# Row normalisation on one core: from two pools of 4-row tiles to an in-place ring of 16-row tiles

## The chip, the core and the metric

The kernel runs on one NeuronCore of one Trainium2 chip. Five engines matter here by name: DVE (the vector engine), ACT (the scalar engine), POOL, SP, which here only issues transfers, and PE, which has no work. Sixteen DMA engines of the core move data between the chip's main memory (HBM) and the core's memory (SBUF, 128 partitions). Two queues feed these sixteen engines: q1 carries what SP issues, q10 what ACT issues.

The metric is the device time of one execution in microseconds; the median of several runs is compared. A profile is one separate execution, and its span runs from the first to the last instruction.

## The reference

```python
batch, seq, dim = 32, 512, 1024            # x is float32

def reference(x, eps):                     # eps = 1e-5
    mean = np.mean(x, axis=-1, keepdims=True)
    var = np.var(x, axis=-1, keepdims=True)
    return ((x - mean) / np.sqrt(var + eps)).astype(np.float32)
```

There are 32 x 512 = 16384 rows of 1024 floats, 4 KB each. Every row is read once and written once: 67.11 MB in and 67.11 MB out.

## The kernel before

A tile is 512 rows, laid out as 128 partitions of K = 4 consecutive rows (line 30), so each partition holds 16 KB that lie together in HBM as well. There are 32 tiles. Two pools of six buffers each hold them: `xin` for what is loaded (line 35) and `yout` for what is stored (line 36). A tile therefore takes 16 KB a partition twice, and up to six tiles may be on their way in and six on their way out.

For each tile, in the loop of line 43:

- SP issues one load of 2 MB (line 47). From the seventh tile on it first waits until the buffer that it reuses is free, which is when DVE and ACT have read the tile six before it.
- DVE makes the statistics (lines 53 and 57): per row two `bn_stats` over 512 elements each and one `bn_aggr`, which gives mean and variance.
- DVE makes minus the mean (line 59), variance plus eps (line 61) and its reciprocal (line 65), each for four rows at once.
- ACT takes the square root of the reciprocal (line 68), which is the factor `rstd`.
- POOL multiplies minus the mean by `rstd` (line 71), which is the offset `nmr`.
- ACT makes the output with one instruction for each row, `yt = xt * rstd + nmr` (line 75), from the input buffer into the output buffer.
- ACT issues one store of 2 MB on its own queue (line 84).

The order on each engine is set by the scheduler of the tile framework, not by the text of the kernel. On ACT it often puts the square root of the next tile, or of the next two, ahead of the four row instructions of a tile. The framework gives each transfer one of eight completion semaphores in turn, and a transfer that reuses a semaphore waits until that semaphore's earlier transfer has landed.

Of the kernel before, what the change touches and what calls it, by code (L numbers as in the profile page):

```python
# [1 line left out]

# [4 lines left out]


@with_exitstack  # L10
def kernel(
    ctx: ExitStack,
    tc: tile.TileContext,
    x: bass.AP,
    eps: bass.AP,
    out: bass.AP,
):
    nc = tc.nc
    P = nc.NUM_PARTITIONS

    eps_val = float(eps) if not isinstance(eps, bass.AP) else 1e-5

    x2 = x.flatten_outer_dims()
    o2 = out.flatten_outer_dims()
    N, D = x2.shape
    BN_MAX = nc.vector.BN_STATS_FMAX
    assert D % BN_MAX == 0
    NSUB = D // BN_MAX

    K = 4  # L30
    rows_per_tile = P * K
    assert N % rows_per_tile == 0
    ntiles = N // rows_per_tile

    xin = ctx.enter_context(tc.tile_pool(name="xin", bufs=6))
    yout = ctx.enter_context(tc.tile_pool(name="yout", bufs=6))
    st = ctx.enter_context(tc.tile_pool(name="st", bufs=4))

    fdt = mybir.dt.float32
    AF = mybir.ActivationFunctionType  # L40
    ALU = mybir.AluOpType

    for t in range(ntiles):
        rows = slice(t * rows_per_tile, (t + 1) * rows_per_tile)

        xt = xin.tile([P, K, D], fdt)
        nc.sync.dma_start(out=xt, in_=x2[rows].rearrange("(p k) d -> p k d", p=P))  # L47

        stats = st.tile([P, K, NSUB, 6], fdt)
        mv = st.tile([P, K, 2], fdt)  # L50
        for k in range(K):
            for s in range(NSUB):
                nc.vector.bn_stats(  # L53
                    out=stats[:, k, s, :],
                    in_=xt[:, k, s * BN_MAX : (s + 1) * BN_MAX],
                )
            nc.vector.bn_aggr(out=mv[:, k, :], in_=stats[:, k, :, :])  # L57
        negmean = st.tile([P, K], fdt)
        nc.vector.tensor_scalar_mul(out=negmean, in0=mv[:, :, 0], scalar1=-1.0)  # L59
        vpe = st.tile([P, K], fdt)  # L60
        nc.vector.tensor_scalar(  # L61
            out=vpe, in0=mv[:, :, 1], scalar1=eps_val, scalar2=None, op0=ALU.add
        )
        ivar = st.tile([P, K], fdt)
        nc.vector.reciprocal(out=ivar, in_=vpe)  # L65

        rstd = st.tile([P, K], fdt)
        nc.scalar.activation(out=rstd, in_=ivar, func=AF.Sqrt, bias=0.0, scale=1.0)  # L68

        nmr = st.tile([P, K], fdt)  # L70
        nc.gpsimd.tensor_mul(out=nmr, in0=negmean, in1=rstd)  # L71

        yt = yout.tile([P, K, D], fdt)
        for k in range(K):
            nc.scalar.activation(  # L75
                out=yt[:, k, :],
                in_=xt[:, k, :],
                func=AF.Identity,
                bias=nmr[:, k : k + 1],
                scale=rstd[:, k : k + 1],  # L80
            )

        dst = o2[rows].rearrange("(p k) d -> p k d", p=P)
        nc.scalar.dma_start(out=dst, in_=yt)


# [1 line left out]
_INS = ['x', 'eps']  # L88
_OUTS = [((32, 512, 1024), 'float32')]
#: Inputs that are plain numbers.  # L90
_NUMBERS = {'eps': 1e-05}


# [26 lines left out]
```

## Time and profile before

| | before |
|---|---|
| runs (three): median, lowest to highest | 321.07 us, 320.96 to 321.11 us |
| profiled execution, span | 319.0 us |
| DVE busy | 181.6 us, 480 instructions |
| ACT busy | 154.3 us, 161 instructions |
| POOL busy | 6.6 us, 36 instructions |
| instructions in all | 926 |
| first `bn_stats` begins | 8.60 us |
| last row instruction of ACT ends | 309.3 us |
| SP's wait at the end for the last stores | part of 57.8 us that it waits for stores, 5 times |

The page of a profile gives the busy time of each engine, then the span in 40 equal slices, then the DMA queues, then the chain of work that ended last (followed back from the last instruction to what released it), then the costliest groups of instructions, and last the transfers by line, with the median time from issue to landing. Of the table, the first and the second row differ by 2.0 us: that lies outside the span, or is the difference between one execution and the others.

### The profile page before, as it was taken

What the parts mean: (1) busy time and instruction counts of PE and PEld (TensorE: products, weight loads), DVE (VectorE), ACT (ScalarE), POOL (GpSimd) and SP (SyncE); (2) the same over time, 40 slices, a digit from 0 to 9 for tenths busy, and PEclk for the clock granted to TensorE, in tenths of its full rate; (3) what the DMA queues carried; (4) which work ended last, traced back from release to release, by engine and by line L of the source; (5) the groups of instructions that cost most, each with busy time, mean ns of one, the idle gap of its engine ahead of it and who ended that gap; (6) DMA issues with size and microseconds to landing.
All of it is one profiled execution on the core that took longest, in us unless ns stands there. A gap on an engine that the chain in (4) does not pass through costs nothing.

```text
span 319.0 us, 926 instructions
## 1 busy us (share of the span) xinstructions
DVE 181.6 (57%) x480; ACT 154.3 (48%) x161; POOL 6.6 (2%) x36
## 2 busy tenths in 40 slices
DVE  0999764457754477544676355765446744467610
ACT  1147491651907419074380833809247091470970
POOL 0000000000000000000000000000000000000000
DMA  7999999999999999999999999999999999999995
GB/s 294 427 405 422 438 431 431 431 429 431 426 429 432 435 431 431 429 427 431 431 433 435 430 431 427 427 431 427 435 438 430 428 431 427 431 427 427 421 427 220
DMA packets 9222, 134.27 MB, mean 421 GB/s; under 512 B 1024, under 2 KB 1024, under 8 KB 1024
## 3 DMA queue, kind: packets, MB, share of 16 engines
q1 hardware_dynamic: 4608, 67.11, 49.6%
q10 hardware_dynamic: 4608, 67.11, 49.2%
q14 instruction: 6, 0.05, 0.0%
HBM read 67.11 MB, written 67.11 MB: 421 GB/s over the span
## 4 chain that ended last, share of the span: by engine, by line
DMA 87%; DVE 4%; issue 3%; ACT 2%; SPq 1%; POOLq 0%; POOL 0%; DVEq 0%
DMA xt<-in_x_dram 87%; DVE stats L53 3%; ACT yt L75 1%; SPq L47 1%; DVE mv L57 0%; DVE ivar L65 0%; DVE negmean L59 0%; POOLq L115 0%; ACT rstd L68 0%; POOL nmr L71 0%; DVE vpe L61 0%; DVEq L65 0%; DVEq L59 0%
## 5 line engine op out<-in xcount | busy, mean ns | idle before, releaser
L53 DVE BATCH_NORM_STATS2 stats<-xt 128x6 f32<-128x512 f32 x256 | 159.4, 665 | 115.3 <-DMA xt<-in_x_dram 115.3
L75 ACT ACTIVATE yt<-xt,nmr,rstd 128x1024 f32<-128x1024 f32 x128 | 146.7, 1227 | 4.7 <-POOL nmr L71 4.5
L68 ACT ACTIVATE rstd<-ivar 128x4 f32<-128x4 f32 x32 | 6.6, 205 | 149.6 <-DVE ivar L65 149.0
L57 DVE BATCH_NORM_AGGREGATE mv<-stats 128x2 f32<-128x12 f32 x128 | 25.1, 196 | 1.1
L71 POOL TENSOR_TENSOR nmr<-negmean,rstd 128x4 f32<-128x4 f32 x32 | 6.3, 198 | 297.9 <-ACT rstd L68 297.9
L65 DVE RECIPROCAL ivar<-vpe 128x4 f32<-128x4 f32 x32 | 5.7, 178 | 3.0
L59 DVE TENSOR_SCALAR negmean<-mv 128x4 f32<-128x4 f32 x32 | 5.4, 170 | 3.1
L61 DVE TENSOR_SCALAR vpe<-mv 128x4 f32<-128x4 f32 x32 | 5.2, 162 | 0.0
L68 ACT ACT_TABLE_LOAD x1 | 1.3, 1283 | 0.7 <-PEq L101 0.7
L101 POOL MEMSET const-float32-0.0<- 128x1 f32 x1 | 0.1, 98 | 0.2 <-issue 0.2
L101 POOL MEMSET const-uint8-127<- 128x1 uint8 x1 | 0.1, 102 | 0.0
L101 POOL MEMSET const-bfloat16-1.0<- 128x1 bf16 x1 | 0.1, 101 | 0.0
L101 POOL MEMSET const-float32-1.0<- 128x1 f32 x1 | 0.1, 98 | 0.0
## 6 DMA issues: line engine op xcount, KB each, us to landing
xt<-in_x_dram SPq DMA_DIRECT2D x32, 2048.0 KB, 38.4
out_dram<-yt ACTq DMA_DIRECT2D x32, 2048.0 KB, 15.5
```

Of the source, the lines that this page charges most:

```text
L47: nc.sync.dma_start(out=xt, in_=x2[rows].rearrange("(p k) d -> p k d", p=P))
L53: nc.vector.bn_stats(out=stats[:, k, s, :], in_=xt[:, k, s * BN_MAX : (s + 1) * BN_MAX],)
L57: nc.vector.bn_aggr(out=mv[:, k, :], in_=stats[:, k, :, :])
L59: nc.vector.tensor_scalar_mul(out=negmean, in0=mv[:, :, 0], scalar1=-1.0)
L61: nc.vector.tensor_scalar(out=vpe, in0=mv[:, :, 1], scalar1=eps_val, scalar2=None, op0=ALU.add)
L65: nc.vector.reciprocal(out=ivar, in_=vpe)
L68: nc.scalar.activation(out=rstd, in_=ivar, func=AF.Sqrt, bias=0.0, scale=1.0)
L71: nc.gpsimd.tensor_mul(out=nmr, in0=negmean, in1=rstd)
L75: nc.scalar.activation(out=yt[:, k, :], in_=xt[:, k, :], func=AF.Identity, bias=nmr[:, k : k + 1], scale=rstd[:, k : k + 1],)
L101: nc = _bacc.Bacc("TRN2", target_bir_lowering=False, num_devices=1)
```

## The change

- The two pools become one buffer `ring` of 48 rows a partition (192 KB), that is three places of 16 rows. ACT writes its result over its input, so a place holds a tile from its load to the end of its store.
- The tiles become 16, 16, 16, 16, 16, 16, 16, 8, 4, 2 and 2 rows a partition, eleven in place of 32. A load of 16 rows is 8 MB and takes 64 KB of consecutive bytes in each partition. The last four tiles share the second place.
- A tile of 16 rows is stored in two halves of 8 rows (4 MB, 32 KB a partition). The smaller tiles are stored whole. That makes 18 stores.
- A load now waits until the stores of the tile that held its place have landed: the load of tile 3 waits for both halves of tile 0, and so on to tile 6. Tile 7 waits for the first half of tile 4 and tile 8 for the second half.
- The statistics are finished by group of four rows (33 groups, the last two of two rows). ACT now takes the square root of variance plus eps directly (the eps comes from a one-column tile that DVE fills at the start). DVE takes the reciprocal of the root and makes the offset in one instruction. POOL has no part in it any more, and two DVE instructions a tile are gone.
- The order on the engines is that of the text: on DVE the reciprocal and the offset of a group stand ahead of the statistics of the next group; on ACT the square root of a group stands behind the four row instructions of the group before, and behind the store issue where one is due.

```diff
+TILES = (16, 16, 16, 16, 16, 16, 16, 8, 4, 2, 2)
+RING = 48
+GROUP = 4
+STORE = 8
...
-    K = 4
-    rows_per_tile = P * K
...
-    xin = ctx.enter_context(tc.tile_pool(name="xin", bufs=6))
-    yout = ctx.enter_context(tc.tile_pool(name="yout", bufs=6))
+    ring_pool = ctx.enter_context(tc.tile_pool(name="ring", bufs=1))
     st = ctx.enter_context(tc.tile_pool(name="st", bufs=4))
+    const = ctx.enter_context(tc.tile_pool(name="const", bufs=1))
...
+    ring = ring_pool.tile([P, RING, D], fdt)
+    eps_t = const.tile([P, 1], fdt)
...
+    def load(t):
+        K, row, pos = plan[t]
+        rows = slice(row * P, (row + K) * P)
+        nc.sync.dma_start(
+            out=ring[:, pos : pos + K, :],
+            in_=x2[rows].rearrange("(p k) d -> p k d", p=P),
+        )
...
+    def group(xt, G):
...
-        negmean = st.tile([P, K], fdt)
-        nc.vector.tensor_scalar_mul(out=negmean, in0=mv[:, :, 0], scalar1=-1.0)
-        vpe = st.tile([P, K], fdt)
-        nc.vector.tensor_scalar(
-            out=vpe, in0=mv[:, :, 1], scalar1=eps_val, scalar2=None, op0=ALU.add
+        nc.scalar.activation(
+            out=std[:, :G], in_=mv[:, :G, 1], func=AF.Sqrt, bias=eps_t, scale=1.0
         )
-        nc.vector.reciprocal(out=ivar, in_=vpe)
-        nc.scalar.activation(out=rstd, in_=ivar, func=AF.Sqrt, bias=0.0, scale=1.0)
-        nc.gpsimd.tensor_mul(out=nmr, in0=negmean, in1=rstd)
-        yt = yout.tile([P, K, D], fdt)
+        nc.vector.reciprocal(out=rstd[:, :G], in_=std[:, :G])
+        nc.vector.scalar_tensor_tensor(
+            out=nmr[:, :G], in0=mv[:, :G, 0], scalar=-1.0, in1=rstd[:, :G],
+            op0=ALU.mult, op1=ALU.mult,
+        )
...
             nc.scalar.activation(
-                out=yt[:, k, :],
+                out=xt[:, k, :],
                 in_=xt[:, k, :],
...
+    def store(t, o, n):
+        K, row, pos = plan[t]
+        rows = slice(row * P, (row + K) * P)
         dst = o2[rows].rearrange("(p k) d -> p k d", p=P)
-        nc.scalar.dma_start(out=dst, in_=yt)
+        nc.scalar.dma_start(
+            out=dst[:, o : o + n, :], in_=ring[:, pos + o : pos + o + n, :]
+        )
...
+    with tc.manual_schedule():
+        nc.vector.memset(eps_t, eps_val)
+        for t, (K, row, pos) in enumerate(plan):
+            load(t)
+            sent = 0
+            for g in range(0, K, GROUP):
+                G = min(GROUP, K - g)
+                group(ring[:, pos + g : pos + g + G, :], G)
+                if g + G - sent >= STORE or g + G == K:
+                    store(t, sent, g + G - sent)
+                    sent = g + G
```

`plan` gives each tile its number of rows, its first row and its position in the ring; a tile that doesn't fit behind the one before begins at position 0 again.

More of the change, by code (lines that the diff above doesn't have):

```diff
@@ L26 @@
     BN_MAX = nc.vector.BN_STATS_FMAX
-    assert D % BN_MAX == 0
     NSUB = D // BN_MAX
-    K = 4
-    rows_per_tile = P * K
-    assert N % rows_per_tile == 0
-    ntiles = N // rows_per_tile
-    xin = ctx.enter_context(tc.tile_pool(name="xin", bufs=6))
-    yout = ctx.enter_context(tc.tile_pool(name="yout", bufs=6))
+    assert sum(TILES) * P == N
+    ring_pool = ctx.enter_context(tc.tile_pool(name="ring", bufs=1))
     st = ctx.enter_context(tc.tile_pool(name="st", bufs=4))
+    const = ctx.enter_context(tc.tile_pool(name="const", bufs=1))
     fdt = mybir.dt.float32
@@ L41 @@
     ALU = mybir.AluOpType
[L43 to L51, printed above, removed]
+    ring = ring_pool.tile([P, RING, D], fdt)
[8 more added lines that the diff above has]
+    def group(xt, G):
+        stats = st.tile([P, GROUP, NSUB, 6], fdt, name="stats")
+        mv = st.tile([P, GROUP, 2], fdt, name="mv")
+        for k in range(G):
             for s in range(NSUB):
@@ L57 @@
             nc.vector.bn_aggr(out=mv[:, k, :], in_=stats[:, k, :, :])
-        negmean = st.tile([P, K], fdt)
-        nc.vector.tensor_scalar_mul(out=negmean, in0=mv[:, :, 0], scalar1=-1.0)
-        vpe = st.tile([P, K], fdt)
-        nc.vector.tensor_scalar(
-            out=vpe, in0=mv[:, :, 1], scalar1=eps_val, scalar2=None, op0=ALU.add
-        )
-        ivar = st.tile([P, K], fdt)
-        nc.vector.reciprocal(out=ivar, in_=vpe)
-        rstd = st.tile([P, K], fdt)
-        nc.scalar.activation(out=rstd, in_=ivar, func=AF.Sqrt, bias=0.0, scale=1.0)
-        nmr = st.tile([P, K], fdt)
-        nc.gpsimd.tensor_mul(out=nmr, in0=negmean, in1=rstd)
-        yt = yout.tile([P, K, D], fdt)
-        for k in range(K):
+        std = st.tile([P, GROUP], fdt, name="std")
+        nc.scalar.activation(
+            out=std[:, :G], in_=mv[:, :G, 1], func=AF.Sqrt, bias=eps_t, scale=1.0
+        )
+        rstd = st.tile([P, GROUP], fdt, name="rstd")
+        nc.vector.reciprocal(out=rstd[:, :G], in_=std[:, :G])
+        nmr = st.tile([P, GROUP], fdt, name="nmr")
+        nc.vector.scalar_tensor_tensor(
+            out=nmr[:, :G],
+            in0=mv[:, :G, 0],
+            scalar=-1.0,
+            in1=rstd[:, :G],
+            op0=ALU.mult,
+            op1=ALU.mult,
+        )
+        for k in range(G):
             nc.scalar.activation(
-                out=yt[:, k, :],
+                out=xt[:, k, :],
                 in_=xt[:, k, :],
@@ L81 @@
             )
+    def store(t, o, n):
+        K, row, pos = plan[t]
+        rows = slice(row * P, (row + K) * P)
         dst = o2[rows].rearrange("(p k) d -> p k d", p=P)
-        nc.scalar.dma_start(out=dst, in_=yt)
+        nc.scalar.dma_start(
+            out=dst[:, o : o + n, :], in_=ring[:, pos + o : pos + o + n, :]
+        )
+    plan = []
+    row = pos = 0
+    for K in TILES:
+        if pos + K > RING:
+            pos = 0
+        plan.append((K, row, pos))
+        row += K
+        pos += K
+    with tc.manual_schedule():
[9 more added lines that the diff above has]
+                    sent = g + G
 _INS = ['x', 'eps']
```

## The prediction

> **What bounds the kernel now.** I read the slices of the page first, then its queues, its chain, its groups, and last a table of stages.
>
> ```profile
> DMA  7999999999999999999999999999999999999995
> GB/s 294 427 405 422 438 431 431 431 429 431 426 429 432 435 431 431 429 427 431 431 433 435 430 431 427 427 431 427 435 438 430 428 431 427 431 427 427 421 427 220
> DMA packets 9222, 134.27 MB, mean 421 GB/s; under 512 B 1024, under 2 KB 1024, under 8 KB 1024
> q1 hardware_dynamic: 4608, 67.11, 49.6%
> q10 hardware_dynamic: 4608, 67.11, 49.2%
> ...
> DMA 87%; DVE 4%; issue 3%; ACT 2%; SPq 1%; POOLq 0%; POOL 0%; DVEq 0%
> ...
> L53 DVE BATCH_NORM_STATS2 stats<-xt 128x6 f32<-128x512 f32 x256 | 159.4, 665 | 115.3 <-DMA xt<-in_x_dram 115.3
> L75 ACT ACTIVATE yt<-xt,nmr,rstd 128x1024 f32<-128x1024 f32 x128 | 146.7, 1227 | 4.7 <-POOL nmr L71 4.5
> ```
>
> The DMA engines are busy in every slice but the first and the last, at about 430 GB/s, and the bytes are fixed by the problem. DVE is idle for 115.3 us before `bn_stats`, always for a load. The two queues have equal shares, and the "under 512 B" count is 64 transfers x 16 engines, so a transfer is 128 pieces of 16 KB (one a partition, 8 an engine) and 16 small completion writes. The table of stages (columns: window, length, DVE, ACT, POOL busy with counts, PEclk, DMA share, GB/s) tells the edges:
>
> ```profile
> 8.00:16.00 8.00, 7.29 (x18) 1.26 (x2) 0.20 (x1) 1.00 0.99 426
> 20.00:22.00 2.00, 2.00 (x6) 0.21 (x1) 0.20 (x1) 1.00 1.02 434
> 22.00:24.00 2.00, 2.00 (x5) 0.00 (x0) 0.00 (x0) 1.00 0.95 311
> 24.00:40.00 16.00, 12.91 (x37) 9.82 (x12) 0.59 (x3) 1.00 1.01 432
> 40.00:280.00 240.00, 137.64 (x362) 119.02 (x124) 4.76 (x24) 1.00 1.01 431
> ...
> 300.00:315.00 15.00, 3.92 (x13) 8.99 (x9) 0.20 (x1) 1.00 0.99 422
> ...
> 315.00:316.00 1.00, 0.00 (x0) 0.00 (x0) 0.00 (x0) 1.00 0.12 49
> 316.00:317.00 1.00, 0.00 (x0) 0.00 (x0) 0.00 (x0) 1.00 0.08 33
> 317.00:318.00 1.00, 0.00 (x0) 0.00 (x0) 0.00 (x0) 1.00 0.04 16
> ```
>
> Loads alone give 426, both directions 431, stores alone 422. The first stores cost a dip (22 to 24 us, 311 GB/s: 0.5 us lost). At the end most engines are done by 315.2 us, but a share of 0.12, 0.08 and 0.04 of sixteen is two engines and then one, until about 317.6. So the span is 134.22 MB / 0.431 MB a us = 311.4 us, about 2.4 us before bytes flow in earnest, some 1 us lost to the dip and the one-way stages, the straggler's 2.5 us, and about 1.5 us to finish. Nothing but the DMA engines is left to shorten.
>
> **What the Trainium skill says.** (1) "DMA: Bandwidth & Descriptors", section "Where 436 GB/s comes from", sets the ceiling at 16 ports x 32 B x 850 MHz = 435.2 GB/s; the trace's 431 is 99.0% of it. (2) Same page, "Why small descriptors are slow (HBM only)": each packet carries a fixed overhead of about 3 cycles beside its 32-byte beats. For 16 KB that is 512 + 3 beats, an estimate of 435.2 x 512/515 = 432.7 GB/s, close to the 431 to 433 that the trace shows with both queues full; larger pieces no run here shows yet. (3) Same page, "Latency and other measured facts": a [128 x 16 KiB] copy at a row pitch of 512 KiB gives 207 GB/s a direction against 214 at full rate, and falls further with larger powers of two. This change raises the pitch between partitions from 16 KB to 64 KB; the trace doesn't show what that does.
>
> **The change part by part.**
>
> *Work per group of four rows.* From the timeline of the first tile, eight `bn_stats` and four `bn_aggr` run from 8.60 to 13.91 us: 5.31 us. Then DVE now waits for ACT: about 0.1 to reach ACT, the root 0.205 (row L68), 0.07 back, the reciprocal 0.178 (L65), 0.05, and the offset, which before doesn't show on DVE; the nearest rows are L59 and L61 at 0.16 to 0.17, and I take 0.17 (bounds 0.1 to 0.3). Sum 6.08, say 6.1 us. Queued behind the waiting reciprocal are the next group's `bn_stats`, and behind those everything of that group. 16384 rows are 32 full groups: 195 us, under the 311 us of the DMA, so it is hidden by DVE's idle 115 us. ACT: four rows 4.63 us (304.71 to 309.34), root 0.2, store issue 0.34 every second group: about 5.1 of each 6.1 us, so the root finds ACT free with about 1 us in hand; if that cover went, each group would be late by the excess, still under the DMA's pace of 9.7 us for four rows. POOL's 6.3 us and DVE's 10.6 us (L59, L61) go: nothing, since both stood beside the DMA. The memset of eps stands before the first load lands: nothing.
>
> *The ring.* A place must be loaded, worked and stored before it is loaded again. Alone, that takes 8.39 MB / 0.431 = 19.5 us, about 2.5 us for issue and landing, first half ready after 2 x 6.1 + 4.7 = 16.9, second after 29.1 us, and 4.19 MB of store 9.7 us with some 2.5 around it: 63 us. The traffic of three places at full rate takes 3 x 38.9 = 117 us. So with three places the DMA queue should hold work for some 53 us more than a turn needs.
>
> *The start.* Three loads (25.2 MB) are queued from 0.73 us and last until 2.4 + 58.4 = 61 us alone. Tile 0 lands at about 23, its halves go out at 40 and 52, tile 1's at about 64 and 76. With the queues sharing evenly the second half of tile 0 has landed at about 82 us; then load 3 starts. By 82 the DMA can have moved 79.6 x 0.431 = 34.3 MB, and 25.2 + 8.4 + 8.4 = 42.0 MB were there to move. It isn't empty. If loads get more than half, load 2 ends near 70, and stores alone fill the time to 82.
>
> *The end.* With even sharing I get tile 6 landed near 240 us, and 16 + 8 + 4 + 2 + 2 rows behind it are 8 groups, 8 x 6.1 = 49 us of DVE; the last store goes out at about 294 us, and the bytes then queued last until about 313. Before, it went out at 309.4 us with 5.5 us to go. Loads finish earlier, stores alone run longer. No gain and no loss but the rate. One wait is odd: by the shared semaphores the second half of tile 5 goes out only when load 6 has landed, which delays it by about 7 us in my schedule; the loads behind it fill the DMA meanwhile.
>
> *The pieces.* Per engine 32 x 8 x 2 = 512 pieces become 11 x 8 + 18 x 8 = 232. By place (2) of the skill, 64 KB (2048 + 3 beats) would run at 434.6 and 32 KB (1024 + 3) at 433.9 GB/s against 432.7: 0.44% for the loads, 0.28% for the stores, mean 0.36% of 311 us, a gain of 1.1 us. Lower bound of the gain: nothing, if with both queues full an engine hides the overhead of one piece behind the other's (share 1.01 and 431 GB/s against 0.99 and 426 for one queue hints at it). Upper bound: the full 435.2, that is 311.4 - 308.4 = 3.0 us. I take 1.1. The one-way stages grow (loads alone to 40 in place of 22 us, stores alone over perhaps 35 in place of 17 us); 36 us more at 1.2 to 2% below would be 0.4 to 0.7 us lost with pieces of 16 KB, but that loss is the overhead of the pieces too and shrinks with them: nothing, at most 0.5. 35 fewer transfers save 35 completion writes an engine, hidden or 0.3 us. These two cancel.
>
> Sum on the profiled execution: 319.0 - 1.1 = 317.9; with the 2.1 us between that span and the median, 320.0 us.
>
> **The rivals.**
>
> *A, the forecast: the DMA stays full, larger pieces save a little.* 318.2 to 320.4, best 320.0. For it: the near match of the overhead estimate with the trace. Chance 0.49.
>
> *B, nothing changes: the overhead is hidden already.* 320.4 to 321.7, best 321.0. For it: shares over 1 with two queues, and the straggling engine that sets the end whatever the pieces. Against it: 431 is below the ceiling. Chance 0.29. It is also the case in which the change does what it says and is worth nothing.
>
> *C, slower: the rate falls with the pitch, in the loads and stores of the seven large tiles.* Place (3) prices a pitch of 512 KiB at 3.3%, which over 311 us is 10 us, 331 us in all. At 64 KB I would expect a fraction: 1% is 3.1 us, less the 1.1 gained, 323.1 us. It decides once the rate is 0.6% down. Against it: the 64 KB that each engine reads are consecutive, and the figure falls off towards small pitches. Chance 0.14.
>
> *D, slower: the DMA runs dry.* If landing a whole 8 MB tile costs far more than my 63 us a turn, say because stores wait behind loads' larger pieces, a turn must pass 117 us before it costs anything; or the last chain of groups is late by more than its 19 us. Each would show as a gap, and a gap of 5 us gives 325 us. Chance 0.08.
>
> **How the numbers follow.** About 0.2% (0.6 us) is what a measurement of this kernel can tell from no change. A gives faster 0.47 and same 0.02; B faster 0.02, same 0.25, slower 0.02; C and D slower 0.20 and same 0.02. In all faster 0.49, same 0.29, slower 0.22. The range begins at A's upper gain, 318.2, and reaches past B into C's likely price, to 323.0; what lies beyond is the dear part of C and most of D, and about 0.05 below.
>
> **What would show it.** Right: 29 x 144, about 4180 packets, in place of 9222, completion writes included, DMA share at 1.0 in all inner slices, rates of 432 to 434 with both queues, first stores near 40 us, the last store issued 10 us or more before the bytes end. Wrong: slices under 425 with a full share (C), slices with a share under 0.97 between 10 and 310 us (D), or the same 431 (B). If the pieces are counted at 16 KB again, the pieces' step falls.

## The result and the profile after

The changed kernel took 321.31 us (median of 4 runs, 320.69 to 322.05) beside 321.09 us before (4 runs, 320.96 to 321.20): ratio 1.0005 with a 95% interval of 0.9987 to 1.0023. In a second set it took 320.60 us (14 runs, 320.11 to 322.27) beside 321.21 us (19 runs): 0.9992, 0.9980 to 1.0005. No change that can be told, with a wider scatter: 18 runs lie between 320.1 and 322.3 us, those before within 0.6 us. The profile below is of the slowest execution, 322.05 us, with a span of 320.3 us.

The page, with the slices of the DMA, its packets and queues, the chain and the two costliest groups:

```profile
span 320.3 us, 721 instructions
...
DMA  9999989999999989999899999999999999999992
GB/s 393 393 401 516 393 327 508 405 393 450 467 385 398 507 372 484 397 393 520 368 422 499 417 393 446 405 459 426 422 450 422 432 426 425 445 438 424 422 417 111
DMA packets 4182, 134.27 MB, mean 419 GB/s; under 512 B 464, under 2 KB 464, under 8 KB 464
...
DMA 56%; DVE 21%; another core or an unknown queue 12%; ACT 3%; issue 1%; SPq 0%
...
L62 DVE BATCH_NORM_STATS2 stats<-ring 128x6 f32<-128x512 f32 x256 | 159.3, 664 | 91.9 <-DMA ring<-in_x_dram 91.9
L83 ACT ACTIVATE ring<-ring,nmr,rstd 128x1024 f32<-128x1024 f32 x128 | 148.4, 1229 | 14.6 <-DVE nmr L74 14.6
```

The packets fell from 9222 to 4182 and the DMA is as full as before. The rates of the slices jump between 327 and 520, and three slices show a share of 0.8, because a piece counts whole in the slice in which it starts: with loads alone, a slice of 8.0 us holds three or four pieces of 64 KB an engine, 393 or 524 GB/s. Over longer stretches the rates are even. The chain now leads through DVE and ACT for a quarter of the span, most of it from 22.7 to 78.3 us, where the first tiles are worked one behind the other, and again behind three later loads; DVE still waits 91.9 us for loads. The same table of stages as before (window, length, DVE, ACT and POOL busy, PEclk, DMA share, GB/s):

```profile
2.00:40.00 38.00, 16.17 (x38) 9.74 (x11) 0.00 (x0) 1.00 0.99 426
40.00:50.00 10.00, 8.99 (x23) 7.16 (x9) 0.00 (x0) 1.00 0.95 365
50.00:60.00 10.00, 9.36 (x23) 7.78 (x8) 0.00 (x0) 1.00 1.08 469
...
110.00:300.00 190.00, 117.32 (x282) 99.06 (x101) 0.00 (x0) 1.00 1.00 432
300.00:313.00 13.00, 0.00 (x0) 0.00 (x0) 0.00 (x0) 1.00 0.98 418
```

Both directions together run at 432; the 426 of the loads alone and the 418 of the stores alone suffer from the same rule of counting at the edges of their windows. When each piece is spread over the time that its record gives it, the loads alone run at 434 GB/s (10 to 40 us), both together at 432 (110 to 300) and the stores alone at 432 (300 to 310). In the kernel before, a longer window with loads alone shows the 431 that it has with both:

```profile
8.00:22.00 14.00, 13.19 (x35) 5.04 (x6) 0.40 (x2) 1.00 1.01 431
```

Now the end, microsecond by microsecond:

```profile
313.00:314.00 1.00, 0.00 (x0) 0.00 (x0) 0.00 (x0) 1.00 0.84 352
314.00:315.00 1.00, 0.00 (x0) 0.00 (x0) 0.00 (x0) 1.00 0.23 98
315.00:316.00 1.00, 0.00 (x0) 0.00 (x0) 0.00 (x0) 1.00 0.14 57
316.00:317.00 1.00, 0.00 (x0) 0.00 (x0) 0.00 (x0) 1.00 0.08 33
317.00:318.00 1.00, 0.00 (x0) 0.00 (x0) 0.00 (x0) 1.00 0.08 33
318.00:319.00 1.00, 0.00 (x0) 0.00 (x0) 0.00 (x0) 1.00 0.04 16
```

Here is where the gain went. Ten of the sixteen engines have stopped by 314.0 us, over a microsecond before those of the kernel before (315.3 to 315.4). But 0.08 of sixteen is about one engine, and its last piece ends at 318.9 us, a microsecond later than the same in the kernel before (317.9). I call such an engine the straggler. Each engine has eight of the 128 pieces of every full transfer, and the others stand idle while it works through what it has left.

The trace also holds the moment at which each engine's part of the last store lands, and the time that each piece takes. I use these below. "Mean end" and "last end" are over the sixteen engines, "lag" is their difference, "booked" is the sum of piece durations per engine, "lengthened" is the part of it that lies above the usual duration of a piece of its size. All in us:

```
                mean end  last end  lag   booked  lengthened  fetches of 8 KB in the run
before           315.91    318.21   2.30  315.20    1.79        6
after            314.86    319.27   4.41  313.25    2.65        6
again            314.70    317.45   2.75  313.28    2.68        6
copy_large       314.59    315.60   1.01  313.31    2.71        0
copy_small       315.20    315.54   0.34  314.90    1.49        0
dve_fetch        315.14    321.04   5.90  313.64    3.05       10
pool_fetch       314.83    317.80   2.97  313.22    2.62       10
few_dve          314.35    316.33   1.98  312.74    2.14        8
before_fetch     318.60    321.51   2.91  315.59    2.19       10
usual duration of a piece: 8 KB 309 ns, 16 KB 611, 32 KB 1213, 64 KB 2418
```

A fetch is a packet of the page's queue "q14 instruction": the engines' own program, read in blocks of 8 KB.

The trace doesn't number the DMA engines, but its records fall into sixteen lists. A piece begins 3 to 4 ns before its predecessor on the same engine ends, and every engine has eight pieces and one completion write of each full transfer. Sorted by these two rules, the records of each trace below give sixteen lists of 8.39 MB. The fetches fit into gaps of the lists, and every one of them, in all these traces, is followed on its list by a lengthened piece, by 0.11 to 0.66 us. "Cost" is 0.30 us a fetch and this lengthening, "others" the median end of the lists without a fetch, in us ("end" is that of a list's last piece; it lands 0.3 to 0.4 us later):

```
              others   DVE's list: end, fetches, cost   POOL's list         a third list
before        315.35   317.89  4  3.31                                      315.96  2  1.08
again         313.81   317.13  4  2.99                                      314.77  2  1.09
dve_fetch     314.12   320.64  8  6.83                                      316.57  2  1.06
pool_fetch    313.90   317.09  4  3.03                  317.48  4  2.34     314.66  2  1.08
before_fetch  318.05   321.18  8  7.09                                      318.05  2  1.10
```

With more instructions on DVE the four fetches more are on one list, together with the four that it has without them: this I call DVE's list, and in all but pool_fetch it ends last. In the first trace of the changed kernel the four come out on two lists, two each, and the two may have been exchanged on the way; its last list ends at 318.91 us, the others at 313.82.

### The profile page after: what moved, and what is told of

Read it like the earlier page. It is cut to its first block, busy times and chain, and to the rows that moved or that the text cites. A ratio compares the mean times of both kernels' runs of the same rounds, so it can differ in the third digit from the quotient of the medians.

```text
span 320.3 us, 721 instructions
## 1 busy us (share of the span) xinstructions
DVE 187.3 (58%) x451; ACT 159.5 (50%) x162; POOL 0.2 (0%) x4
## 2 busy tenths in 40 slices
DMA packets 4182, 134.27 MB, mean 419 GB/s; under 512 B 464, under 2 KB 464, under 8 KB 464
## 4 chain that ended last, share of the span: by engine, by line
DMA 56%; DVE 21%; another core or an unknown queue 12%; ACT 3%; issue 1%; SPq 0%
DMA ring<-in_x_dram 42%; DVE stats L62 17%; DMA out_dram<-ring 14%; DVE mv L66 3%; ACT ring L83 2%; ACT std L68 1%; DVE rstd L72 1%; DVE nmr L74 1%; SPq L52 0%
## 5 line engine op out<-in xcount | busy, mean ns | idle before, releaser
L62 DVE BATCH_NORM_STATS2 stats<-ring 128x6 f32<-128x512 f32 x256 | 159.3, 664 | 91.9 <-DMA ring<-in_x_dram 91.9
L83 ACT ACTIVATE ring<-ring,nmr,rstd 128x1024 f32<-128x1024 f32 x128 | 148.4, 1229 | 14.6 <-DVE nmr L74 14.6
L68 ACT ACTIVATE std<-mv,eps_t 128x4 f32<-128x4 f32 (+1 forms) x33 | 9.8, 297 | 125.1 <-DVE mv L66 125.1
L66 DVE BATCH_NORM_AGGREGATE mv<-stats 128x2 f32<-128x12 f32 x128 | 26.7, 209 | 4.4
L72 DVE RECIPROCAL rstd<-std 128x4 f32<-128x4 f32 (+1 forms) x33 | 5.8, 177 | 12.0 <-ACT std L68 12.0
L74 DVE SCALAR_TENSOR_TENSOR nmr<-mv,rstd 128x4 f32<-128x4 f32 (+1 forms) x33 | 5.4, 162 | 1.1
```

What stands on the lines that cost most here:

```text
L62: nc.vector.bn_stats(out=stats[:, k, s, :], in_=xt[:, k, s * BN_MAX : (s + 1) * BN_MAX],)
L68: nc.scalar.activation(out=std[:, :G], in_=mv[:, :G, 1], func=AF.Sqrt, bias=eps_t, scale=1.0)
L72: nc.vector.reciprocal(out=rstd[:, :G], in_=std[:, :G])
L74: nc.vector.scalar_tensor_tensor(out=nmr[:, :G], in0=mv[:, :G, 0], scalar=-1.0, in1=rstd[:, :G], op0=ALU.mult, op1=ALU.mult,)
L83: nc.scalar.activation(out=xt[:, k, :], in_=xt[:, k, :], func=AF.Identity, bias=nmr[:, k : k + 1], scale=rstd[:, k : k + 1],)
```

## The experiments

My theory (S) was that the large pieces do save what was forecast, and that one straggling DMA engine takes it back. The rival (R) was that the rate is no better with large pieces. Under S I had two causes for the straggler: instruction fetches, or the uneven starts of queues. "Starting a queue" means that a first transfer begins on it while the other queue is at work.

**again.** The changed kernel unaltered, to have a second trace.

> The changed kernel once more, for a second trace and more times. Theory S (straggler: on average the 16 DMA engines end about 1 us earlier than before, but one engine ends 4 us after that average, 2 us before the change): the runs scatter between 320.6 and 322.1 us, and a run with an earlier end has a last engine that lags less, while the mean of the engines' ends stays near 314.9 us. Theory R (the rate itself is no better with large pieces): the mean of the ends moves with the time.

320.60 us, and the profiled run, 320.25 us, ends with its last engine at 317.45 in place of 319.27 us, while the mean end moved by 0.16 to 314.70. So the time of these two runs follows the last engine, as S has it. The lists say where the 1.8 us between them lie, with the same six fetches in both. Fetches and lengthened pieces together are 7.3 us on the last list of the first trace and 5.6 us on that of the second, beside 2.2 and 2.4 us on the median list. Most of the difference lies in pieces that began between 80 and 100 us, around the start of load 3: 1.9 us of lengthening against 0.5. In the second trace such a burst (1.7 us) fell on a list without fetches. What decides which engine it hits, no run shows.

**copy_large.** No statistics and no row instructions.

```diff
-                group(ring[:, pos + g : pos + g + G, :], G)
```

> The changed kernel without the statistics and without the row instructions: it only copies, so all arithmetic is left out; loads, stores, ring and their waits stay. It has almost no instructions to fetch while it runs. Theory S with instruction fetches as its cause: the last engine lags the mean by under 1 us in place of 4.4, and the time falls to about 317.5 us. Theory S with the starts of queues as the cause: the lag stays above 2 us, time 319 to 321. Theory R: mean of the ends as before or later, time 321 or more. If compute were still bounding a stretch: below 316 us.

318.39 us (5 runs, 317.56 to 320.63), ratio to before 0.9926 (0.9897 to 0.9955). The mean end is within 0.3 us of that with all the work (314.59 against 314.86 and 314.70), so compute bounds next to nothing; the lag is 1.0 us. The end of this copy:

```profile
313.00:314.00 1.00, 0.00 (x0) 0.00 (x0) 1.00 0.97 410
314.00:315.00 1.00, 0.00 (x0) 0.00 (x0) 1.00 0.14 57
315.00:316.00 1.00, 0.00 (x0) 0.00 (x0) 1.00 0.00 0
```

All sixteen engines stop within 1.4 us. Without a program to fetch there is hardly a straggler in this execution. But two of the five runs took 319.71 and 320.63 us, 1.3 and 2.2 us more, with nothing to fetch either, so fetches are not all of it. In these runs such scatter goes with the ring: the changed kernel spreads over 2.2 us, the kernel before and its copy over 0.6 and 0.5 us.

**copy_small.** The kernel before without its arithmetic: loads, stores of the same buffer, pieces of 16 KB. The lines of the arithmetic, which go too, are not shown.

```diff
-    xin = ctx.enter_context(tc.tile_pool(name="xin", bufs=6))
+    xin = ctx.enter_context(tc.tile_pool(name="xin", bufs=12))
...
-        nc.scalar.dma_start(out=dst, in_=yt)
+        nc.scalar.dma_start(out=dst, in_=xt)
```

> The kernel before without the statistics and the row instructions (all arithmetic left out), with twelve buffers in the one pool that loads and stores now share; the pieces are 16 KB as before. Against the copy with large pieces it prices the pieces alone: 280 pieces an engine at 4 to 5 ns are 1.1 to 1.4 us that this one should be longer in the mean of the engines' ends. Theory R expects no difference. Theory S by fetches: last engine under 1 us behind the mean, time about 318.5 us.

318.64 us (4 runs), mean end 315.20, lag 0.34. Against the large pieces the mean end is 0.61 us later, half of what I expected for 280 pieces. The table shows why: the large pieces' booked time is 1.6 us less although 1.2 us more of it is lengthening. Starting a queue lengthens the pieces in flight; that returns part of what fewer pieces save. The rest of the way from 1.6 to 0.61 us is overlap: pieces overlap by some 4 ns each, and with 280 fewer of them about 1.1 us of it goes (an estimate from these records).

**dve_fetch.** More instructions for DVE to fetch, without work that anyone waits for.

```diff
+        junk = st.tile([P, 1], fdt, name="junk")
+        for k in range(16):
+            nc.vector.memset(junk, 0.0)
```

> The changed kernel with 16 tiny memsets more on DVE in each of the 33 groups, 528 instructions of about 0.06 us, behind the offset; nothing waits for their result but DVE itself, 32 us of its 92 idle ones. Four 8 KB instruction fetches more are expected. Theory S by fetches: each takes 0.31 us of one DMA engine and makes the last engine later, by 1.2 us in all (lag about 5.6 us, time about 322.5). Theory S by queue starts, and theory R: no more than 0.3 us.

323.54 us (4 runs), 2.9 us above the unaltered kernel. Four more fetches, as expected, at 0.73 us each rather than 0.31. The pages of both name them, first the unaltered kernel's

```profile
q14 instruction: 6, 0.05, 0.0%
```

and then this one's, with its last microseconds:

```profile
q14 instruction: 10, 0.08, 0.1%
```

```profile
315.00:316.00 1.00, 0.00 (x0) 0.00 (x0) 0.00 (x0) 1.00 0.14 57
316.00:317.00 1.00, 0.00 (x0) 0.00 (x0) 0.00 (x0) 1.00 0.10 41
317.00:318.00 1.00, 0.00 (x0) 0.00 (x0) 0.00 (x0) 1.00 0.06 25
318.00:319.00 1.00, 0.00 (x0) 0.00 (x0) 0.00 (x0) 1.00 0.06 25
319.00:320.00 1.00, 0.00 (x0) 0.00 (x0) 0.00 (x0) 1.00 0.06 25
320.00:321.00 1.00, 0.00 (x0) 0.00 (x0) 0.00 (x0) 1.00 0.04 16
```

A share of 0.06 is one engine of sixteen, alone for over three microseconds; the mean end moved by 0.4. What was made longer is that engine's list of work: its eight fetches cost it 6.8 us where four cost 3.0. DVE's own time is not the cause: the last store went out at 305.49 us, in place of 299.35, still some 8 us before most engines ran out of bytes.

**pool_fetch.** The same memsets on POOL (`nc.gpsimd.memset`).

> The changed kernel with the same 528 tiny memsets more, but on POOL, which has no other work; nothing waits for them. If what made the run with the memsets on DVE 2.9 us longer was the fetching of instructions in general, by the same DMA engine, this one is as much longer (323 to 324 us). If each compute engine fetches through a DMA engine of its own, the last engine's lag stays at 2.8 to 4.4 us and the time at 320.6 to 321.3, while another engine of the sixteen falls behind by 2 to 4 us. If DVE's own time was the cause: no change.

320.75 us (20 runs) against the unaltered kernel's 320.60: no change, with the same ten fetches. (Beside 321.14 us before, in 43 runs, the ratio is 0.9990, 0.9983 to 0.9997: with this many runs a gain of 0.1% shows.) In this trace the second-last engine ends at 317.47 us (315.98 in the run again) and the last at 317.80 (317.45). So POOL's fetches don't lengthen the list of the engine that was last; another one has fallen behind to near it. The lists show it: POOL's four fetches are on a list without any of DVE's, at a cost of 2.3 us, and that list ends 0.4 us behind DVE's. So POOL's fetches were not free; they fell on an engine that had room.

**few_dve.** The reverse: fewer instructions on DVE. Mean and variance are put together from the results of `bn_stats` by twelve small POOL instructions a group (396 in 33 groups; the expectation below miscounts them as 13), and a group is finished one group later within its tile.

```diff
-            nc.vector.bn_aggr(out=mv[:, k, :], in_=stats[:, k, :, :])
...
+        v = nc.gpsimd
+        for h in range(2):
+            v.tensor_add(out=a[:, :G, :, h], in0=q[:, :G, 0:2, 1 + h], in1=q[:, :G, 2:4, 1 + h])
+        v.tensor_add(out=b[:, :G], in0=a[:, :G, 0, :], in1=a[:, :G, 1, :])
...
+        nc.scalar.activation(out=std[:, :G], in_=var4[:, :G], func=AF.Sqrt, bias=eps_t, scale=0.25)
         nc.vector.reciprocal(out=rstd[:, :G], in_=std[:, :G])
-        nc.vector.scalar_tensor_tensor(
+        v.tensor_mul(out=nmr[:, :G], in0=nm[:, :G], in1=rstd[:, :G])
```

> The changed kernel with bn_aggr, and the offset, replaced by 13 small POOL instructions a group of four rows (the same mean and variance from the same bn_stats); of DVE only bn_stats and the reciprocal are left, 290 instructions in place of 451, and a group is finished one group later within its tile. Theory S by fetches of DVE: 161 fewer instructions are about 1.3 fetches fewer, at 0.73 us each (2.9 us over four in the run with 528 more) about 0.9 us less: 319.7 us, last engine under 2 us behind the mean; POOL's own fetches go through another engine, as in the run with POOL memsets. If the lag had another cause: 320.6 us.

320.29 us (10 runs, 319.24 to 321.06) beside 321.28 us before (15 runs): ratio 0.9971 (0.9960 to 0.9982). This is faster than the kernel before beyond its interval; against the changed kernel's 320.60 it is 0.3 us in the medians, measured in another set and within the scatter. The gain is less than the 0.9 us expected. The traced run is the fastest of the ten, 319.24 us. Its page, and its end:

```profile
DVE 157.6 (50%) x290; ACT 157.9 (50%) x162; POOL 74.9 (24%) x400
```

```profile
314.00:315.00 1.00, 0.00 (x0) 0.00 (x0) 0.00 (x0) 1.00 0.25 106
315.00:316.00 1.00, 0.00 (x0) 0.00 (x0) 0.00 (x0) 1.00 0.14 57
316.00:317.00 1.00, 0.00 (x0) 0.00 (x0) 0.00 (x0) 1.00 0.00 0
```

The last two engines end together, at 316.32 and 316.33 us: by the lists one of them has three fetches (2.6 us) and the other none, but 4.3 us of lengthened pieces against 1.7 on the median list. So there would be little more to win by moving instructions.

**before_fetch.** 512 memsets more on DVE in the kernel before, to see whether a fetch costs less where pieces are small.

```diff
         nc.vector.reciprocal(out=ivar, in_=vpe)
+        junk = st.tile([P, 1], fdt)
+        for k in range(16):
+            nc.vector.memset(junk, 0.0)
```

> The kernel before (pieces of 16 KB) with 16 tiny memsets more on DVE for each of its 32 tiles, 512 instructions, about four fetches more, as in the run that gave 2.9 us with large pieces; DVE then has some 30 of its 115 idle us less. It tells why the last engine lags more after the change than before (4.4 and 2.8 us in two profiles, 2.3 before) though both fetch six times. If a fetch costs its engine more where the pieces in flight are large: 0.3 to 0.45 us each here, 1.2 to 1.8 us in all, 322.3 to 322.9 us. If a fetch costs the same with any pieces: 0.73 us each, 324.1 us, and the larger lag after the change comes from the starts of queues instead.

324.51 us (4 runs), 3.4 us above before, 0.84 us a fetch: as much as with large pieces, so the first expectation falls. Here the lag itself grew little, 2.91 us, because the other engines became late too:

```profile
296.00:300.00 4.00, 0.94 (x5) 2.48 (x4) 0.20 (x1) 1.00 0.54 225
300.00:304.00 4.00, 3.03 (x6) 4.00 (x5) 0.00 (x0) 1.00 1.04 442
```

The straggler's part of the last load came late, 7.2 us behind the fifteenth engine's, so the last tile began late, and the other fifteen ran out of stores for about 2 us. (In the kernel before it was 3.1 us behind.) The straggler was never idle near the end (its parts of the last five stores landed 4.9 us apart, eight pieces of 0.61 us), so its own list of work is what grew by 3.3 us.

**ramp.** First tiles of 2, 2, 4 and 8 rows, so that the first stores begin early, with small pieces in flight.

```diff
-TILES = (16, 16, 16, 16, 16, 16, 16, 8, 4, 2, 2)
+TILES = (2, 2, 4, 8, 16, 16, 16, 16, 16, 16, 8, 4, 2, 2)
```

> The changed kernel with tiles of 2, 2, 4 and 8 rows ahead of six of 16, then 8, 4, 2, 2 (fourteen tiles): the first stores begin near 12 us, with small pieces in flight. Theory: starting a queue lengthens the pieces in flight in proportion to their size; in the changed kernel that cost 2.7 us an engine against 1.8 before. Here it should be 1.5 to 2, so the engines' mean end falls to about 314 and the time to about 320.0 us. If starts cost the same whatever is in flight: no change, 320.6.

321.51 us (22 runs, 319.7 to 325.6): a miss. The lengthening was 2.51 us, not 1.5 to 2: smaller where the first stores begin, but the start of a load after 80 us cost as before (0.6 us an engine). The wide scatter isn't explained.

**eights.** Fifteen tiles of 8 rows in the same ring.

```diff
-TILES = (16, 16, 16, 16, 16, 16, 16, 8, 4, 2, 2)
+TILES = (8,) * 15 + (4, 2, 2)
```

> The changed kernel with fifteen tiles of 8 rows and then 4, 2, 2 in the same ring: pieces of 32 KB in both directions, six places, and the load queue should not run empty again after the start. Loads lose 0.3 us an engine to smaller pieces, starts of queues gain about 1 us. Expected 320.0 us; if the large pieces are what counts, 321.0.

324.41 us (6 runs), ratio 1.0093 (1.0061 to 1.0126): a miss in the other direction. The lengthening is 6.0 us an engine, in bursts of 0.2 to 0.9 us every 20 us or so, while I had thought that the load queue would never run empty. And the end has a hole:

```profile
310.00:314.00 4.00, 2.85 (x6) 0.18 (x1) 0.00 (x0) 1.00 0.97 414
314.00:316.00 2.00, 0.33 (x2) 1.57 (x3) 0.00 (x0) 1.00 0.57 242
316.00:318.00 2.00, 0.00 (x0) 0.92 (x1) 0.00 (x0) 1.00 0.27 115
318.00:320.00 2.00, 0.00 (x0) 0.00 (x0) 0.00 (x0) 1.00 0.96 397
```

Fifteen engines' parts of the last tile's load had landed by 306.1 us, the straggler's only at 310.4, and the store of that tile had next to nothing before it: 0.43 and 0.73 of two microseconds each, 2.3 us, are lost.

**before_eights.** The kernel before with tiles of 8 rows and half as many buffers: larger pieces alone.

```diff
-    K = 4
+    K = 8
...
-    xin = ctx.enter_context(tc.tile_pool(name="xin", bufs=6))
-    yout = ctx.enter_context(tc.tile_pool(name="yout", bufs=6))
+    xin = ctx.enter_context(tc.tile_pool(name="xin", bufs=3))
+    yout = ctx.enter_context(tc.tile_pool(name="yout", bufs=3))
```

> The kernel before with K = 8 and three buffers in each pool in place of 4 and six: pieces of 32 KB, the two pools, the scheduler's order and the buffer bytes stay. It does one part of the change alone. By the pieces the mean of the engines' ends should come 0.6 us earlier than in the kernel before (256 in place of 512 pieces), DVE has 48 instructions fewer; against that the last tile is 8 rows: its last store goes out about 10 us later than the last load's landing and the bytes may run out, 2 to 4 us. Expected 321 to 324 us. If pieces were all, 320.4.

324.69 us (4 runs), 0.7 us beyond the range expected; ratio 1.0106 (1.0091 to 1.0120). Its booked time is 313.22 us, as low as with the change, but the bytes run out before the last tile is through:

```profile
296.00:298.00 2.00, 2.00 (x5) 0.00 (x0) 0.00 (x0) 1.00 0.65 279
298.00:300.00 2.00, 2.00 (x6) 0.00 (x0) 0.00 (x0) 1.00 0.04 16
300.00:302.00 2.00, 0.84 (x5) 0.56 (x2) 0.20 (x1) 1.00 0.27 115
```

About 4 us are lost there. So large pieces alone didn't pay here; the change has stores in halves and a last tile of two rows beside them, and its bytes don't run out. Which of the two it needs, no run separates.

**shift15.** The last 256 rows cut into 16 on 16 partitions and 240 on 120 partitions, to take work off one DMA engine.

> The changed kernel with its last tile of 256 rows cut into 16 rows on 16 partitions and 240 rows on 120 partitions, which by the Trainium skill (DMA: Bandwidth & Descriptors, section on why a DMA increments its semaphore by 16) should run on the 15 lowest DMA engines: the sixteenth has 15 rows less each way, about 4.5 us less. If the straggler is that one, the last engine's lag goes, and the time falls to about 319 us. If it is another, the time stays at 320.6 or rises by up to 0.6.

324.82 us (4 runs), a miss on both branches. The trace has 494 completion writes in place of 464: the 32 of the tile that was cut up go, 32 come for the load and the store on 16 partitions and 30 for those on 120, so these did run on 15 engines. Four engines ended at 316.4, 318.4, 320.6 and 322.8 us; probably the two uneven transfers made stragglers of their own, which no run shows. Which engine the straggler is stays open.

## Why the prediction came out as it did

The forecast was 320.0 us by case A, with B (no change, 321.0 us) second. The medians, 321.31 and 320.60 us, lie in what B was given, and the measurement can't tell them from no change. But B's reason, that the overhead is hidden already, is not what happened: the overhead was there and most engines saved it, and one engine gave it back. By steps:

- *The bound.* Right. Taking all the arithmetic away leaves the mean end within 0.3 us. One reading on the way was not: the 426 GB/s and the share of 0.99 with loads alone came from the edges of the window. The longer window above shows 431 and 1.01, as with both queues, so the hint for B that was drawn from the difference, that one queue's overhead hides behind the other's, falls with it.
- *A group of four rows, 6.1 us.* 6.36 us (22.66 to 29.02). The larger part of the miss is the statistics, 5.71 us in place of 5.31: in the order of the text each `bn_aggr` follows straight on its row's `bn_stats`, while the scheduler of the kernel before had put a `bn_stats` of the next row between them. The root takes 0.297 us in place of the 0.205 I took over, the offset 0.162 of my 0.17, and the hand-overs less than I allowed. Hidden, as said.
- *The start.* Stores foreseen at 40 and 52 us went out at 40.16 and 52.87. Load 3, foreseen at 82, was issued at 82.58 us. Of the two cases the loads had more than half: only stores ran just before. The places never ran the DMA dry (D): with each piece spread over its time, the share is 1.00 or 1.01 in every stretch of 10 us from 10 to 310 us.
- *The end.* The last store went out at 299.98 us in place of 294, with bytes until 314 for most engines: still covered. The odd wait came as foreseen: the second half of tile 5 went out at 234.24 us, when load 6 had landed, 9 us after its rows were done (7 foreseen).
- *The pieces, 1.1 us.* Right in size for the sum, in part by luck. The mean end came 1.05 us earlier (1.21 in the second trace), but between the two copies, which differ in little but the pieces and the ring, it is 0.61 us. Some 0.35 us of the rest, by an estimate, are time in which the engines of the kernel before had less to do: from 280 to 310 us their share is 0.99 to 1.00 in place of 1.01 (each piece spread over its time), because the straggler's parts of the last loads came late. What is left isn't shown. The durations give the cost of a piece: from 8 to 64 KB they grow by 2109 ns for 57344 bytes, which is 27.19 GB/s an engine or 435.0 in all, and about 8 ns stay for each piece, of which some 4 overlap with the next. That is the ceiling of 435.2 GB/s, and the 4 ns left are close to the 3 cycles a packet that the prediction took from the Trainium skill ("DMA: Bandwidth & Descriptors", "Why small descriptors are slow (HBM only)"), since 3 beats in 515 are 3.6 of a 16 KB piece's 611 ns (an estimate). What the sum left out here is the lengthening, 2.65 us an engine against 1.79, most of it where queues start.
- *The step that kept A from coming true* is the sum's silent assumption that the straggler's 2.5 us stay as they are. The straggler ends the span, and its lag was 4.41 us in one trace and 2.75 in the other against 2.30. The prediction named it under B ("the straggling engine that sets the end whatever the pieces") but gave it no price. The runs price it: 0.7 to 0.8 us for each block of instructions that DVE fetches, with pieces of either size. That makes the straggler, but not its growth, since the fetches are as many as before and cost as much (3.3 us before, 3.0 after). What grew is the lengthening that falls unevenly on the engines when loads of 64 KB start among stores: 0.5 us on most lists and 1.6 to 1.9 us on the latest two in the trace with a lag of 4.41 us, and nothing in those 20 us of the kernel before. The copies, which fetch nothing, show growth as well (lag 1.01 against 0.34 us, one trace each). How much of it the straggler gets differs from run to run, and in the second trace it was none beyond the others; why stays open.
- *C, the pitch.* Not seen: with both directions 432 GB/s against 431 before. The signs set for C and D, slices under 425 GB/s or with a share under 0.97, do appear in the page, but only from counting a piece whole where it starts.

## What to carry to other kernels

When the DMA engines are full from end to end, read the last microseconds one by one: a share of 0.06 is one engine of sixteen, and it, not the mean rate, sets the time. A change that gains on the mean is worth only what the last engine gains. Number and size of the pieces were worth 0.6 to 1 us in 320 here, and a tail that doesn't keep stores queued behind the last load cost 2 to 4 us.

## What I had not expected of the hardware

- The program itself travels through the DMA engines that carry the data. 528 instructions of 0.06 us on DVE, which has 92 us to spare, cost 2.9 us; the same 528 on POOL changed the time by nothing that could be measured, since their fetches fell on another DMA engine. The fetch's own record is 0.309 us, the cost some 0.7 to 0.8 us; the difference is in the piece right behind it on the same engine, which takes 0.11 to 0.66 us longer than usual (0.49 us in the mean of the ten fetches of dve_fetch).
- Starting a queue lengthens the pieces in flight on the other one: around the first stores, at 40 us, by 1.06 us an engine with loads of 64 KB, and at 20 us in the kernel before by 0.54 us with 16 KB. It is no plain proportion: with 32 KB it was 1.35 us in before_eights, and with 16 KB 0.77 us in copy_small.
